# Chunk 7 of the attention scored inside the key/value loop, with the cached keys, score banks, buffers and ScalarE's order set for it

## The chip, the cores and the metric

The kernel runs on one core of a Trainium2 chip. The metric is the device time of one launch in microseconds. The engines named below are TensorE (PE in the profile, its weight loads PEld), VectorE (DVE), ScalarE (ACT), GpSimd (POOL) and SyncE (SP, which here only issues DMAs). Each engine works through its own list of instructions in order; between engines, semaphores order the work.

## The reference

One inference step of a two-layer model over 1024 prompt rows and 32 sample rows of width 1024. Layer 0 is an mLSTM mixer, layer 1 attention in a band of chunks; each is followed by an MLP. The change touches the place where layer 1 begins: keys and values are computed once from the stream, and each chunk of 64 queries attends to its own chunk and the eight before it, with a learned bias by relative position.

```python
kv = (x * (1 + kv_scale) + kv_shift) @ p['w_kv']
k_sh = kv[..., :KV_W].reshape(Bsz, S, NKV_B, HD_B)
v_sh = kv[..., KV_W:].reshape(Bsz, S, NKV_B, HD_B)
q = (u @ p['w_q_b'][lb]).reshape(Bsz, S, NH_B, HD_B)
...
def one_chunk(args):
    ci, qb = args
    kb = lax.dynamic_slice_in_dim(kp, ci * CHUNK, span, axis=1)
    vb = lax.dynamic_slice_in_dim(vp, ci * CHUNK, span, axis=1)
    s = jnp.einsum('bqkgd,bskd->bkgqs', qb, kb).astype(jnp.float32) * (HD_B ** -0.5) + bias
    valid = (ci * CHUNK - BAND + jnp.arange(span)) >= 0
    s = jnp.where(valid, s, -jnp.inf)
    p = jax.nn.softmax(s, axis=-1).astype(vb.dtype)
    return jnp.einsum('bkgqs,bskd->bqkgd', p, vb)
```

There are 16 query heads in 4 key groups of 4. The 32 sample rows attend to 512 cached keys and their own 32.

## The kernel before

**Precision.** Products are taken on values split into a high and a low part (hi and lo); ScalarE writes the hi part by a rounding cast, VectorE the lo part as a difference (`split`, L89 and L90).

**The key/value loop.** `for t in range(NT)` runs over 9 blocks of rows: 8 of 128 prompt rows and one of the 32 sample rows (t = 8). For each block, `kv_input(t)` loads the normed rows from DRAM (L1728), scales and shifts them on GpSimd (L1733) and VectorE (L1734) and splits them into `uk_t` (L89, L90). Two blocks are always prepared ahead. TensorE then multiplies: 24 matmuls for the keys (`kv0_t`) and 24 for the values (`kv1_t`), three at a time (L1755 hi by hi, L1756 hi by lo, L1757 lo by hi), into banks of PSUM that `bank()` hands out in rotation.

**Keys into place.** `put_keys` takes a block of keys: it splits them (`kd`, L1702 ScalarE, L1703 VectorE), then, at the next tick of the `flow`, transposes them on TensorE (`kt`, L1708, four matmuls into one bank) and copies them to the two forms of the key buffer `k` (L1713; four copies on ScalarE, then four on VectorE). New keys are named kt_n, the cached ones kt_c. `cached_keys(c)` loads a block of 128 cached keys and values, yields, and hands over to `put_keys`; the loop adds one of its four blocks at t = 0, 2, 4 and 6. `flow` is a list of such generators, and `flow.tick()`, called twice a block, moves them on. For t >= 4 the block's keys and values are also written out (`ks`, L1766 to L1770).

**The attention.** Only after the loop are the bias tiles loaded (bias0 to bias3, L1787 and L1791), and the order of work is a list, `todo`: for each pair of key groups `gp`, chunks alternate between wide ones (9 chunks of keys) and slim ones, beginning with chunk 8, then 7, 12, 6. Each entry is a `Group` of one chunk and one key group `e`. A group has two units (two query heads of 64 queries each make 128 rows). A unit is: scores on TensorE (`s`, L1805), the bias added and the row's extreme taken on VectorE (L1815, then a read of its accumulator), exp on ScalarE (L1818). Then per group a reciprocal of the sums (L1824 VectorE), the two units normalized on GpSimd (L1826), their transposes on TensorE (`pt`, L1840) and copies to `pT` that alternate between ScalarE (L1849) and VectorE (L1851). When both groups of a chunk are there, `pv` multiplies by the values (L1862), and the result goes back, split again, into `QO` (L1867, L1868).

In round n of the loop, group n is scored, group n - 1 normalized, group n - 3 transposed and group n - 4 multiplied by the values. Two score buffers rotate (tag `s`, `bufs=2`), three for `pt`, one for `pv`. TensorE's order in this loop is as written (`manual_schedule`); elsewhere, and on the other engines, a scheduler orders the instructions by its own estimate, within what the data and the buffers allow. Softmax tiles `p` take their place from three pools in a rotation of 12 counted by `nun`; the x tiles of `kv_input` use one of these pools (`raw_tile`) too.

## Time and profile before

| | |
|---|---|
| median of 3 runs | 2427.9 us (2427.4 to 2428.0) |
| profiled execution | 2430.0 us, its span 2427.9 us |
| TensorE's clock, mean over the span | 0.993 of full |
| key/value loop, from block 2 to the last transposes | about 1361 to 1411 us of the span |
| attention begins with the scores of chunk 8 | 1412.4 us |

Times in the profile are counted from the span's start. A row of the windows view gives, for a stretch, the busy microseconds of PE, PEld, DVE, ACT and POOL with the number of instructions in brackets, then the granted TensorE clock, the busy share of the DMA engines and GB/s. A row of the timeline gives start, duration, engine, line, operation, output and inputs, how many instructions it sums up, and in square brackets the idle time before it with what ended it. A row of the waits view gives who waited for whom: microseconds in total, times, longest. A row of the groups view gives the count, busy us and mean ns of one, then the idle time of the engine just before.

### The profile page before, as it was taken

The numbers are of one execution on the slowest core, as the hardware profiler recorded it, in microseconds if no ns is written. First come the engines' busy times: TensorE is split into PE (matmuls) and PEld (weight loads), VectorE is DVE, ScalarE is ACT, GpSimd is POOL, SyncE is SP. The second block draws the span as 40 slices with busy tenths as digits, with TensorE's granted clock in tenths as the row PEclk, the third lists the DMA queues.
The fourth block names the chain that finished last, engine by engine and source line by source line (L and its number), as shares of the span: only waits on it lengthen the run. The fifth ranks groups of instructions, "written<-read, shape, count | busy, mean of one in ns | idle before, by whom it ended". The sixth has DMA issues, their size and how long they took to land.

```text
span 2427.9 us, 44306 instructions
## 1 busy us (share of the span) xinstructions
PE 2361.4 (97%) x17180; PEld 2265.5 (93%) x17180; DVE 1973.8 (81%) x4094; ACT 1180.5 (49%) x2394; POOL 166.5 (7%) x315
## 2 busy tenths in 40 slices
PE   7999999999999999999999999999999999899997
PEld 4999999999999999999989977789999999899997
DVE  4899897778788789989887666756998888887878
ACT  4544456278566630000147466764776777222212
POOL 0111100000000000000001124420000000000003
PEclk9999999999999999999999999999999999999999
DMA  8432322436556896576413220042586779966642
GB/s 295 124 112 87 108 81 90 161 109 206 183 184 203 290 345 244 211 263 216 162 62 100 69 70 1 10 121 57 168 279 222 257 259 337 367 245 235 228 149 72
DMA packets 283702, 423.60 MB, mean 174 GB/s; under 512 B 15320, under 2 KB 205164, under 8 KB 278372
## 3 DMA queue, kind: packets, MB, share of 16 engines
q1 hardware_dynamic: 279460, 390.50, 48.3%
q10 hardware_dynamic: 4032, 30.28, 3.1%
q8 instruction: 135, 2.21, 0.4%
q14 instruction: 75, 0.61, 0.1%
HBM read 304.91 MB, written 118.17 MB: 174 GB/s over the span
## 4 chain that ended last, share of the span: by engine, by line
PE 50%; DVE 10%; DMA 4%; ACT 4%; issue 2%; POOL 1%; SPq 0%; ACTq 0%; DVEq 0%; POOLq 0%
PE dn L1424 11%; PE up L1289 8%; PE dn L120 4%; PE dn L119 4%; PE dn L118 4%; PE pv L1862 3%; PE s L1805 2%; PE pt L1840 2%; DMA radw<-in_w_ada_dram 2%; PE op_b L118 1%; PE op_b L119 1%; DVE wf_u L90 1%; PE op_b L120 1%; DMA rdn_u<-in_w_up_dram 1%; PE up L120 1%
## 5 line engine op out<-in xcount | busy, mean ns | idle before, releaser
L1054 DVE SCALAR_TENSOR_TENSOR ACX<-dn,ada,ACX 128x264 f32<-128x264 f32 (+6 forms) x664 | 281.5, 447 | 84.6 <-PE dn L1424 41.3
L1424 PE MATMUL dn<-fx,wf_d 128*128 128x264 f32 x2016 | 254.0, 285 | 6.4 <-DVE ACX L1054 4.0
L1424 PEld LDWEIGHTS dn<-fx,wf_d 128*128 128x128 f32 x2016 | 248.7, 188 | 8.7 <-DVE ACX L1054 2.7
L89 ACT CAST w_dn<-raw_dn 128x1024 fp32r<-128x1024 f32 x36 | 37.7, 1051 | 284.0 <-DMA raw_dn<-in_w_down_dram 133.1
L118 PE MATMUL dn<-hs,w_dn 128*128 128x384 f32 (+2 forms) x512 | 161.0, 315 | 0.0
L119 PE MATMUL dn<-hs,w_dn 128*128 128x384 f32 (+2 forms) x512 | 160.9, 315 | 0.0
L120 PE MATMUL dn<-hs,w_dn 128*128 128x384 f32 (+2 forms) x512 | 156.4, 314 | 1.3 <-DVE w_dn L90 1.3
L1289 PE MATMUL up<-TF,wf_u 128*128 128x264 f32 x1056 | 143.4, 285 | 3.8 <-ACT H L1292 3.8
L1289 PE MATMUL up<-U,wf_u 128*128 128x264 f32 x1056 | 140.1, 285 | 2.5 <-DVE H L1295 2.0
L1289 PE MATMUL up<-u,wf_u 128*128 128x264 f32 x1056 | 139.7, 285 | 1.6 <-ACT wf_u L89 0.6
L277 DVE SCALAR_TENSOR_TENSOR aw<-radw,cs,aw 128x512 f32<-128x512 f32 x196 | 139.3, 743 | 0.8 <-DMA radw<-in_w_ada_dram 0.8
L1289 PEld LDWEIGHTS up<-TF,wf_u 128*128 128x128 f32 x1056 | 134.2, 188 | 5.1 <-ACT H L1292 5.1
L1289 PEld LDWEIGHTS up<-U,wf_u 128*128 128x128 f32 x1056 | 133.1, 188 | 4.0 <-DVE H L1295 3.0
L1289 PEld LDWEIGHTS up<-u,wf_u 128*128 128x128 f32 x1056 | 132.6, 188 | 2.5 <-ACT wf_u L89 0.8
L119 PE MATMUL dn<-U,w_dn 128*128 128x384 f32 (+2 forms) x416 | 129.8, 313 | 0.0
L118 PE MATMUL dn<-U,w_dn 128*128 128x384 f32 (+2 forms) x416 | 129.4, 312 | 0.3 <-DVE ada L302 0.3
L120 PE MATMUL dn<-U,w_dn 128*128 128x384 f32 (+2 forms) x416 | 125.5, 312 | 0.6 <-DVE w_dn L90 0.6
L120 PEld LDWEIGHTS dn<-hs,w_dn 128*128 128x128 f32 x512 | 95.9, 188 | 2.1 <-DVE w_dn L90 1.7
L119 PEld LDWEIGHTS dn<-hs,w_dn 128*128 128x128 f32 x512 | 96.5, 188 | 0.0
L118 PEld LDWEIGHTS dn<-hs,w_dn 128*128 128x128 f32 x512 | 96.4, 188 | 0.1
L1815 DVE CUSTOM_DVE_ANT_0 p<-s,bias 128x576 f32<-128x576 f32 (+9 forms) x132 | 79.1, 605 | 20.2 <-PE s L1805 13.4
L90 DVE TENSOR_TENSOR HL<-H,HL 128x1056 fp32r<-128x1056 f32 x64 | 80.3, 1254 | 17.5 <-ACT HL L89 17.5
(394 smaller groups left out, 7167.5 us busy)
## 6 DMA issues: line engine op xcount, KB each, us to landing
hpl<-HL SPq DMA_DIRECT2D x144, 264.0 KB
rdn_u<-in_w_up_dram SPq DMA_DIRECT2D x64, 512.0 KB
hd<-HL SPq DMA_DIRECT2D x28, 1056.0 KB
fx<-hd SPq DMA_DIRECT2D x50, 528.0 KB
radw<-in_w_ada_dram SPq DMA_DIRECT2D x24, 1024.0 KB
hd<-HM SPq DMA_DIRECT2D x28, 792.0 KB
raw_up<-in_w_up_dram SPq DMA_DIRECT2D x40, 512.0 KB
raw_dn<-in_w_down_dram SPq DMA_DIRECT2D x36, 512.0 KB
```

The lines of the kernel that those rows point to most:

```text
L90: (eng or nc.vector).tensor_sub(dst_l, src, dst_h.bitcast(F32))
L118: nc.tensor.matmul(ps, wh, mov(0, k), start=(k == 0), stop=False)
L119: nc.tensor.matmul(ps, wh, mov(1, k), start=False, stop=False)
L120: nc.tensor.matmul(ps, wl, mov(0, k), start=False, stop=(k == nk - 1))
L277: nc.vector.scalar_tensor_tensor(acc[cnd], raw[:, k], sc, acc[cnd], op0=ALU.mult, op1=ALU.add)
L1054: nc.vector.scalar_tensor_tensor(xs, ps[:, off + o:off + o + mm_], gate[:, fc, cnd:cnd + 1], xs, op0=ALU.mult, op1=ALU.add)
L1289: nc.tensor.matmul(p, self.ws[w][:, wl, k], moving(f, tp, xl, k), start=first and k + n_ == 0, stop=k == 3 and n_ == 2, skip_group_check=n ...
L1424: nc.tensor.matmul(p, ws[w][:, wl, k], t[:, s0, xl], start=first and k + n_ == 0, stop=k == kg - 1 and n_ == 2, skip_group_check=not first)
L1805: nc.tensor.matmul(s[:, b, :w], qst, kk[i][:, g, k0 + j0:k0 + j0 + w], start=(i == 0), stop=(i == 1))
L1815: nc.vector.tensor_tensor_reduce(out=z.rearrange("p (b w) -> p b w", b=np_), in0=s[:, :np_, :w], in1=bt.rearrange("p (b w) -> p b w", b=np ...
L1840: nc.tensor.transpose(pt[:kp, j - j0, pr * P:(pr + 1) * P], ps_[pr][:, j * P:j * P + kp], ident)
L1862: nc.tensor.matmul(pv[64 * e:64 * e + 64, :nq], V[:kp, vt0 + j, g * 64:(g + 1) * 64], pts[e][:kp, j, :nq], start=(j == 0), stop=(j == nt - 1))
```

## The change

Chunk 7 becomes the first entry of `todo`, ahead of chunk 8, and its two groups are scored inside the key/value loop: group 0 ahead of block 7's matmuls and group 1 ahead of block 8's, through `early`. Their scores go to PSUM banks of the loop (`bank`), and their bias comes from two new tiles (`near_bias`), loaded at t = 6 into buffers of `raw_tile`. Group 0 is normalized in the second call. After the loop the rounds start at n = 2.

```diff
-        yield 3.0
+        yield 4.0
         yield from put_keys(cr, P, TP + t * P, f"c{t}")
...
+    nun, near, groups = [7], {}, {}
+    bank_n[0] += 6
...
+        s = bank(f"s_{nm}")[:, None] if near else psT.tile([P, 2, 512], F32, tag="s", name=f"s_{nm}", bufs=2)
...
+            bt = near[self.e][:, pr] if near else \
+                bias[2 * self.g + pr][:, 576 - self.nk:] if self.c < 16 else sbias[self.g]
...
+            if not gp and i < 2:
+                c = 7 + i
...
+    def near_bias(e):
+
+        b = raw_tile([P, 2, 512], f"near_{e}")
+        for hd in range(2):
+            nc.sync.dma_start(b[64 * hd:64 * hd + 64],
+                              bias_d[4 * e + hd:4 * e + hd + 3:2, :, 64:576].rearrange("h i j -> i h j"))
+        return b
+
+    def early(n):
+
+        groups[n] = Group(*todo[n][:3])
+        for pr in range(2):
+            groups[n].scores(pr)
+        if n:
+            normalize(groups[0].units, groups[0].mx)
+
     for t in range(NT):
-        if t % 2 == 0 and t < 8:
-            flow.add(cached_keys(t // 2))
+        if t in (0, 1, 3, 4):
+            flow.add(cached_keys((0, 1, 3, 4).index(t)))
+        if t >= NT - 2:
+            early(t - NT + 2)
...
+        if t == NT - 3:
+            near.update({e: near_bias(e) for e in range(2)})
+        if t >= NT - 3:
+            bias_load(t - NT + 3)
     flow.finish()
+    near.clear()
+    nun[0] = 4
     ps0.__exit__(None, None, None)
+    bias_load(3)
...
     with tc.manual_schedule(engines={mybir.EngineType.PE}):
-        for n in range(len(todo) + 4):
-            new, old, done = n if n < len(todo) else None, groups.get(n - 3), groups.pop(n - 4, None)
-            if done and done.e:
+        act_order = tc.manual_schedule(engines={mybir.EngineType.PE, mybir.EngineType.Activation})
+        act_order.__enter__()
+        for n in range(2, len(todo) + 4):
+            if n == 6:
+                act_order.__exit__(None, None, None)
+            new, done = n if n < len(todo) else None, groups.pop(n - 4, None)
+            old = groups.get(n - 2 if n < 4 else n - 3) if n != 4 else None
+            if done and done.e and n > 5:
                 done.values()
             if new is not None:
                 groups[n] = Group(*todo[n][:3])
                 groups[n].scores(0)
+            if n == 4:
+                groups[1].values()
```

The functions of the attention (`softmax_unit`, `normalize`, `transposed`, `weighted_values`, `Group`) are moved as they stand to a place ahead of the loop, and the loads of the bias tiles become `bias_load(i)`, three of which are called at t = 6, 7 and 8. The cached keys are taken up at t = 0, 1, 3 and 4, with a yield of 4.0 in place of 3.0. `bank_n[0] += 6` shifts the rotation of the banks, and `nun` starts at 7 and is set to 4 after the loop, with which the softmax tiles of chunk 12 and later take the same pools as before. In rounds 2 to 5 ScalarE's order too is as written. The matmuls of the attention and of the loop are the same in number and shape.

VectorE's list around the third and fourth block of keys, before (kd1 is the lo part of a key block, c for cached and n for new, the number the block; k1 the copies to the second key buffer; uk and x the loop's inputs by block):

```order
L1734 TENSOR_TENSOR x1_5_15192<-x1_5_15192,kvss_14864 128x1024
L90 TENSOR_TENSOR uk_3_15024<-x1_3_15022,uk_3_15024 128x1024
L1703 TENSOR_TENSOR kd1_n2_15110<-kv0_2_15029,kd0_n2_15109 128x256
L1713 CAST k1_14842<-kt_c0_15055 64x2x128 x4
L1713 CAST k1_14842<-kt_n1_15068 64x2x128 x4
L1703 TENSOR_TENSOR kd1_c1_15185<-ck_1_15081,kd0_c1_15184 128x256
L90 TENSOR_TENSOR uk_4_15115<-x1_4_15113,uk_4_15115 128x1024
```

and now:

```order
L1734 TENSOR_TENSOR x1_5_15211<-x1_5_15211,kvss_14864 128x1024
L90 TENSOR_TENSOR uk_3_15026<-x1_3_15024,uk_3_15026 128x1024
L1703 TENSOR_TENSOR kd1_c0_15058<-ck_0_14914,kd0_c0_15057 128x256
L1713 CAST k1_14842<-kt_n1_15061 64x2x128 x4
L1703 TENSOR_TENSOR kd1_n2_15113<-kv0_2_15031,kd0_n2_15112 128x256
L90 TENSOR_TENSOR uk_4_15118<-x1_4_15116,uk_4_15118 128x1024
L1713 CAST k1_14842<-kt_c0_15099 64x2x128 x4
```

The lo part of the cached block c0, which stood several rows ahead of x1_5, now stands behind the split of uk_3, and its copies follow two rows later than those of n1. On TensorE the transposes kt_c0 stood between block 2's key and value matmuls; they now stand directly ahead of block 3's first matmul.

TensorE's list where the loop ends and the attention begins, before (kt_n8 is the last key block, s_0_8_00 the scores of group pair 0, chunk 8, group 0, unit 0):

```order
L1708 MATMUL kt_n8_15634<-ident_64,kd0_n8_15626 128x32 x2
L1708 MATMUL kt_n8_15634<-ident_64,kd1_n8_15627 128x32 x2
L1805 MATMUL s_0_8_00_15675<-k0_14841,QO1_14267 128x288
L1805 MATMUL s_0_8_00_15675<-k1_14842,QO1_14267 128x288
...
L1805 MATMUL s_0_8_01_15683<-k0_14841,QO1_14267 128x288
...
L1805 MATMUL s_0_8_10_15692<-k0_14841,QO1_14267 128x288
...
L1805 MATMUL s_0_7_10_15728<-k0_14841,QO1_14267 128x512
L1805 MATMUL s_0_7_10_15728<-k1_14842,QO1_14267 128x512
L1840 MATMUL pt_0_8_0_0_15738<-ident_64,p_0_8_00_15680 128x128
```

and now:

```order
L1708 MATMUL kt_n8_15685<-ident_64,kd0_n8_15670 128x32 x2
L1708 MATMUL kt_n8_15685<-ident_64,kd1_n8_15671 128x32 x2
L1776 MATMUL s_0_8_00_15712<-k0_14841,QO1_14267 128x288
L1776 MATMUL s_0_8_00_15712<-k1_14842,QO1_14267 128x288
...
L1811 MATMUL pt_0_7_0_0_15724<-ident_64,p_0_7_00_15506 128x128
L1811 MATMUL pt_0_7_0_0_15724<-ident_64,p_0_7_01_15512 128x128
...
L1776 MATMUL s_0_8_01_15730<-k0_14841,QO1_14267 128x288
...
L1811 MATMUL pt_0_7_0_2_15738<-ident_64,p_0_7_00_15506 128x128
```

Before, seven score units stood ahead of the first transposes; now the transposes of chunk 7 stand between the score units of chunk 8.

VectorE's list at the same place, before:

```order
L1703 TENSOR_TENSOR kd1_n8_15627<-kv0_8_15549,kd0_n8_15626 32x256
L1713 CAST k1_14842<-kt_c3_15575 64x2x128 x4
L1713 CAST k1_14842<-kt_n7_15588 64x2x128 x4
L1713 CAST k1_14842<-kt_n8_15634 64x2x32 x4
L1815 ISA p_0_8_00_15680,mx_0_8_0_15674<-s_0_8_00_15675,bias0_15654 128x576
L1815 ISA mx_0_8_0_15674 128x1
L1815 ISA p_0_8_01_15688,mx_0_8_0_15674<-s_0_8_01_15683,bias0_15654 128x576
```

and now:

```order
L1786 ISA p_0_7_10_15594,mx_0_7_1_15590<-s_0_7_10_15591,near_1_15496 128x512
...
L1786 ISA p_0_7_11_15600,mx_0_7_1_15590<-s_0_7_11_15597,near_1_15496 128x512
...
L1795 RECIPROCAL mx_0_7_1_15590<-mx_0_7_1_15590 128x2
L1703 TENSOR_TENSOR kd1_n8_15671<-kv0_8_15606,kd0_n8_15670 32x256
L1713 CAST k1_14842<-kt_n7_15632 64x2x128 x4
L1713 CAST k1_14842<-kt_n8_15685 64x2x32 x4
L1786 ISA p_0_8_00_15717,mx_0_8_0_15711<-s_0_8_00_15712,bias0_15499 128x576
```

The copies of the cached block c3 have left this place for an earlier one, and the reads of chunk 7's last scores now stand ahead of the last key block's lo part.

More of the change, by code (lines that the diff above doesn't have):

```diff
@@ L1743, in cached_keys, with bias_load @@
         nc.sync.dma_start(V[:, 8 + t], cv[t * P:(t + 1) * P])
-        yield 3.0
+        yield 4.0
         yield from put_keys(cr, P, TP + t * P, f"c{t}")
-    for t in range(NT):
-        if t % 2 == 0 and t < 8:
-            flow.add(cached_keys(t // 2))
-        m = P if t < NT - 1 else TS
-        uk = uks[t]
-        pk = [bank(f"kv{i}_{t}")[:, :256] for i in range(2)]
-        for i in range(2):
-            for k in range(KC):
-                w = wkv[i][k // 4]
-                nc.tensor.matmul(pk[i], uk[:, 0, k], w[:, 0, k % 4], start=(k == 0), stop=False)
-                nc.tensor.matmul(pk[i], uk[:, 0, k], w[:, 1, k % 4], start=False, stop=False)
-                nc.tensor.matmul(pk[i], uk[:, 1, k], w[:, 0, k % 4], start=False, stop=(k == KC - 1))
-            if i == 0:
-                flow.tick()
-        vi = t if t < NT - 1 else 12
-        nc.scalar.copy(V[:m, vi], pk[1][:m])
-        flow.add(put_keys(pk[0][:m], m, t * P if t < NT - 1 else TP + 512, f"n{t}"))
-        flow.tick()
-        if t >= 4:
-            ks = tmp_t([P, 256], f"ks_{t}")
-            nc.scalar.copy(ks[:m], pk[0][:m])
-            dk, dv = (o["k_p"], o["v_p"]) if t < NT - 1 else (o["k_s"], o["v_s"])
-            r0 = (t - 4) * P if t < NT - 1 else 0
-            nc.sync.dma_start(dk[0, r0:r0 + m].rearrange("s g d -> s (g d)"), ks[:m])
-            nc.sync.dma_start(dv[0, r0:r0 + m].rearrange("s g d -> s (g d)"), V[:m, vi])
-        if t + 2 < NT:
-            uks.append(kv_input(t + 2))
-    flow.finish()
-    ps0.__exit__(None, None, None)
     at_cm = tc.tile_pool(name="attn", bufs=1, reuse_waits="tile")
     at = at_cm.__enter__()
-    psT_cm = tc.tile_pool(name="psT", bufs=1, space=PSUM, reuse_waits="tile")
-    psT = psT_cm.__enter__()
     bias, sbias = [], []
-    for i, (nb, ns) in enumerate(((3, 0), (3, 0), (2, 1), (0, 3))):
+    def bias_load(i):
+        nb, ns = ((3, 0), (3, 0), (2, 1), (0, 3))[i]
         bt = ring.tile([P, 2112], F32, tag="wc", name=f"bias{i}", bufs=6)
@@ L1792, in trunk_kernel @@
                               bias_d[h0:h0 + 4 * ns - 3:4, :32, :544].rearrange("h i j -> i h j"))
-        bias += [b3[:, j] for j in range(nb)]
-        sbias += [s3[:, j] for j in range(ns)]
-    nun = [0]
+        bias.extend(b3[:, j] for j in range(nb))
+        sbias.extend(s3[:, j] for j in range(ns))
+    nun, near, groups = [7], {}, {}
+    bank_n[0] += 6
     def softmax_unit(qst, g, k0, nk, bt, off, mx, nm):
-        s = psT.tile([P, 2, 512], F32, tag="s", name=f"s_{nm}", bufs=2)
+        s = bank(f"s_{nm}")[:, None] if near else psT.tile([P, 2, 512], F32, tag="s", name=f"s_{nm}", bufs=2)
         parts = [(0, 0, nk)] if nk <= 512 else [(0, 0, nk // 2), (1, nk // 2, nk // 2)]
@@ L1888, in scores @@
                 return
-            bt = bias[2 * self.g + pr][:, 576 - self.nk:] if self.c < 16 else sbias[self.g]
+            bt = near[self.e][:, pr] if near else \
+                bias[2 * self.g + pr][:, 576 - self.nk:] if self.c < 16 else sbias[self.g]
             self.units.append(softmax_unit(qo(self.c)[:, self.e, self.gp, pr * P:(pr + 1) * P], self.g, self.k0, self.nk,
@@ L1920, in trunk_kernel @@
             c = slim[gp][i // 2] if i % 2 else wide[i // 2] if i < 16 else slim[gp][8]
+            if not gp and i < 2:
+                c = 7 + i
             todo += [(gp, c, e, gp and e and i in (8, 11)) for e in range(2)]
-    groups = {}
-    with tc.manual_schedule(engines={mybir.EngineType.PE}):
-        for n in range(len(todo) + 4):
-            new, old, done = n if n < len(todo) else None, groups.get(n - 3), groups.pop(n - 4, None)
-            if done and done.e:
+    def near_bias(e):
[4 more added lines that the diff above has]
+        return b
@@ new lines, in early @@
+    def early(n):
[4 more added lines that the diff above has]
+            normalize(groups[0].units, groups[0].mx)
+    for t in range(NT):
+        if t in (0, 1, 3, 4):
+            flow.add(cached_keys((0, 1, 3, 4).index(t)))
+        if t >= NT - 2:
+            early(t - NT + 2)
+        m = P if t < NT - 1 else TS
+        uk = uks[t]
+        pk = [bank(f"kv{i}_{t}")[:, :256] for i in range(2)]
+        for i in range(2):
+            for k in range(KC):
+                w = wkv[i][k // 4]
+                nc.tensor.matmul(pk[i], uk[:, 0, k], w[:, 0, k % 4], start=(k == 0), stop=False)
+                nc.tensor.matmul(pk[i], uk[:, 0, k], w[:, 1, k % 4], start=False, stop=False)
+                nc.tensor.matmul(pk[i], uk[:, 1, k], w[:, 0, k % 4], start=False, stop=(k == KC - 1))
+            if i == 0:
+                flow.tick()
+        vi = t if t < NT - 1 else 12
+        nc.scalar.copy(V[:m, vi], pk[1][:m])
+        flow.add(put_keys(pk[0][:m], m, t * P if t < NT - 1 else TP + 512, f"n{t}"))
+        flow.tick()
+        if t >= 4:
+            ks = tmp_t([P, 256], f"ks_{t}")
+            nc.scalar.copy(ks[:m], pk[0][:m])
+            dk, dv = (o["k_p"], o["v_p"]) if t < NT - 1 else (o["k_s"], o["v_s"])
+            r0 = (t - 4) * P if t < NT - 1 else 0
+            nc.sync.dma_start(dk[0, r0:r0 + m].rearrange("s g d -> s (g d)"), ks[:m])
+            nc.sync.dma_start(dv[0, r0:r0 + m].rearrange("s g d -> s (g d)"), V[:m, vi])
+        if t + 2 < NT:
+            uks.append(kv_input(t + 2))
+        if t == NT - 3:
+            near.update({e: near_bias(e) for e in range(2)})
+        if t >= NT - 3:
+            bias_load(t - NT + 3)
@@ new lines, in trunk_kernel @@
+    flow.finish()
+    near.clear()
+    nun[0] = 4
+    ps0.__exit__(None, None, None)
+    bias_load(3)
+    psT_cm = tc.tile_pool(name="psT", bufs=1, space=PSUM, reuse_waits="tile")
+    psT = psT_cm.__enter__()
+    with tc.manual_schedule(engines={mybir.EngineType.PE}):
+        act_order = tc.manual_schedule(engines={mybir.EngineType.PE, mybir.EngineType.Activation})
[6 more added lines that the diff above has]
+            if done and done.e and n > 5:
```

## The prediction

> **What bounds the kernel now.** I read first the page's busy shares:

> ```profile
> PE 2361.4 (97%) x17180; PEld 2265.5 (93%) x17180; DVE 1973.8 (81%) x4094; ACT 1180.5 (49%) x2394; POOL 166.5 (7%) x315
> ```

> TensorE is busy for 97% of the span, so a change that leaves its work alone can win only where it idles or where its clock is not full. The change issues the same attention matmuls as before; only their places differ. So I looked for idle and slow clock near those places, in windows of 3.41 us laid on the steps at which the granted clock changes (PE, PEld, DVE, ACT, POOL busy with counts, then the clock, DMA share and GB/s):

> ```profile
> 1368.53:1371.94 3.41, 1.65 (x14) 1.45 (x13) 3.35 (x6) 1.57 (x3) 0.00 (x0) 1.00 0.04 9
> 1371.94:1375.36 3.42, 3.42 (x19) 3.42 (x18) 3.32 (x8) 0.37 (x1) 0.06 (x1) 0.50 0.55 151
> ...
> 1409.49:1412.90 3.41, 1.88 (x17) 1.67 (x16) 3.27 (x10) 2.21 (x9) 0.00 (x0) 1.00 0.43 70
> 1412.90:1416.32 3.42, 3.42 (x15) 2.95 (x13) 2.64 (x9) 1.74 (x4) 0.00 (x0) 0.50 0.92 211
> 1416.32:1419.73 3.41, 1.82 (x6) 0.90 (x6) 1.83 (x6) 2.03 (x5) 1.48 (x2) 1.00 1.04 240
> 1419.73:1423.14 3.41, 3.41 (x15) 2.83 (x13) 1.84 (x8) 2.34 (x7) 1.47 (x3) 0.50 1.07 252
> 1423.14:1426.56 3.42, 0.96 (x8) 0.75 (x8) 1.43 (x4) 2.23 (x6) 2.73 (x4) 1.00 0.27 57
> 1426.56:1429.97 3.41, 3.41 (x18) 2.79 (x18) 1.87 (x4) 0.95 (x2) 0.00 (x0) 0.50 0.00 0
> ...
> 1569.92:1573.33 3.41, 2.49 (x18) 1.59 (x18) 1.91 (x9) 2.55 (x8) 2.42 (x4) 1.00 0.00 0
> 1573.33:1576.75 3.42, 3.42 (x30) 3.25 (x30) 3.34 (x11) 2.78 (x9) 1.06 (x6) 1.00 0.00 0
> ```

> The entry to attention, 1409.49 to 1429.97, holds three such pairs. Idle: (3.41 - 1.88) + (3.41 - 1.82) + (3.42 - 0.96) = 5.6 us. Slow clock: (3.42 + 3.41 + 3.41) / 2 = 5.1 us. Together 10.7 us, and the view of waits names what the idle time waited for:

> ```profile
> PE pt L1840 <- POOL p L1826: 2.5, 1, 2.5
> PE s L1805 <- DVE mx L1815: 1.6, 2, 0.8
> PE s L1805 <- DVE k L1713: 1.5, 1, 1.5
> ```

> The 1.5 is the first score matmul waiting for the last key copies to leave a PSUM bank, the 1.6 two waits for a score buffer that VectorE has not read, and the 2.5 the first transposes waiting for the first softmax. They are the start of a pipeline with nothing yet to fill it.

> **The change part by part.** *The entry, what is removed.* Chunk 7 is now scored inside the key/value loop and its four softmax units are through VectorE, ScalarE and, for the first half, GpSimd before the loop ends. Its transposes are then ready work between the scores of chunk 8, and the first score tile stands on a bank that the last key copies do not hold. The three waits lose their causes: -10.7 us if no window falls to half.

> *The entry, what is left.* VectorE still has to read four score tiles. What TensorE does until then, and how long VectorE takes, from the steady rounds (timeline of PE, then groups from 1430 to 1613 us):

> ```profile
> 1432.72 0.60 PE L1840 MATMUL pt<-ident,p 128*128 128x128 f32 x4
> 1433.07 0.77 PE L1805 MATMUL s<-k,QO 128*128 128x288 f32 x4
> 1433.68 0.60 PE L1840 MATMUL pt<-ident,p 128*128 128x128 f32 x4
> ```

> ```profile
> L1826 POOL TENSOR_SCALAR p<-p,mx 128x576 f32<-128x576 f32 x60 | 44.1, 749 | 56.4 <-DVE mx L1824 56.4
> L1815 DVE CUSTOM_DVE_ANT_0 p<-s,bias 128x576 f32<-128x576 f32 x58 | 43.6, 753 | 3.2 <-PE pt L1840 1.4 <-PE s L1805 0.7
> L1851 DVE COPY pT<-pt 128x512 f32<-128x512 f32 x38 | 26.0, 683 | 0.9 <-PE pt L1840 0.4
> L1815 DVE DVE_READ_ACCUMULATOR2_ANT mx<- 128x1 f32 x120 | 9.9, 82 | 0.0
> L1824 DVE RECIPROCAL mx<-mx 128x2 f32<-128x2 f32 x59 | 9.7, 164 | 17.6 <-ACT p L1818 17.1
> ```

> By their starts a score unit takes TensorE 1433.68 - 1433.07 = 0.61 us and a pair of transposes 1433.07 - 1432.72 = 0.35. After the last key transposes TensorE has five score units and four pairs before it needs chunk 7's second pT in its first pv: 5 x 0.61 + 4 x 0.35 = 4.5 us. VectorE's queue up to that pT holds the new row's key copies, four reads, two pT copies and a reciprocal:

> ```profile
> 1408.80 1.73 DVE L1713 CAST k<-kt_c 64x256 fp32r<-64x256 f32 x4 [1.12 <-ACT k L1713]
> 1410.54 2.69 DVE L1713 CAST k<-kt_n 64x256 fp32r<-64x256 f32 x8
> 1410.45 0.43 PE L1708 MATMUL kt_n<-ident,kd_n 32*128 32x32 f32 x4
> ```

> The eight casts take 2.69 us, a block's four alone 1.73, so the new row's four take 0.96. The queue is 0.96 + 4 x (0.753 + 0.082) + 2 x 0.683 + 0.164 = 5.8 us, 1.3 more than TensorE's 4.5. That holds if VectorE stands free when the last transposes are done. Before, block 7's casts still ran to 1410.54 + 1.73 = 1412.27 there, 1.4 us after 1410.45 + 0.43; in the change the cached block's 1.73 us is out of their way, but two reads of chunk 7 lie there instead, so I take the middle of 1.3 and 2.7: 2.0 us. Two later waits of a pipeline still short are likely, for a bank of chunk 12's scores (a read, 0.84 at most) and for chunk 8's second normalize on GpSimd (0.75 at most); half of each is 0.8. Left over: 2.8 us, spread in pieces under 1.7, so no window should halve. Bounds: 0 (copies and reads hidden behind TensorE) and 5.6 (every microsecond of the old idle comes back, without its clock). ScalarE's fixed order costs nothing by itself: in the windows above it is busy at most 2.34 of 3.41 us.

> *The third block of keys.* Cached keys now come in at blocks 0, 1, 3 and 4, and tick four units late. The keys c0 move behind the split of uk_3 on VectorE and their transposes from the middle of block 2 to its end. TensorE already stands there:

> ```profile
> 1368.11 1.23 DVE L1734 TENSOR_TENSOR x<-x,kvss 128x1024 f32<-128x1024 f32 x1 [4.18 <-POOL x L1733]
> 1369.25 1.22 DVE L90 TENSOR_TENSOR uk<-x,uk 128x1024 fp32r<-128x1024 f32 x1
> 1370.50 0.42 DVE L1703 TENSOR_TENSOR kd_n<-kv,kd_n 128x256 fp32r<-128x256 f32 x1
> ```

> ```profile
> 1364.63 0.60 PE L1708 MATMUL kt_c<-ident,kd_c 128*128 128x128 f32 x4
> 1365.07 0.60 PE L1708 MATMUL kt_n<-ident,kd_n 128*128 128x128 f32 x4
> 1368.37 0.28 PE L1755 MATMUL kv<-w_kv,uk 128*128 128x256 f32 x1
> 1368.49 0.28 PE L1756 MATMUL kv<-w_kv,uk 128*128 128x256 f32 x1
> 1370.53 0.39 PE L1757 MATMUL kv<-w_kv,uk 128*128 128x256 f32 x1 [1.76 <-DVE uk L90]
> ```

> The stall ended with uk_3's split. Now it ends with c0's difference behind that split (0.42, the kd_n row's shape), and on its far side then lie the transposes kt_c0 (1365.07 - 1364.63 = 0.44) and block 3's first two matmuls (2 x 0.12 by their starts), which ran ahead of it before. Added: 0.42 + 0.44 + 0.24 = 1.1 us. The window behind it is at half clock either way. Bounds: 0 (uk_3 comes as much earlier), and 1.1 + 1.7 = 2.8 (the longer stall empties parts of two windows).

> *The moved scores and their bias.* Chunk 7's eight score matmuls leave the entry for the loop: what they add there they took there, 0. Their VectorE reads, four of at most 0.84 us, lie where VectorE has room: it was busy 1.09 of 3.41 us in the window 1406.08 to 1409.49:

> ```profile
> 1406.08:1409.49 3.41, 3.41 (x31) 3.41 (x31) 1.09 (x3) 2.52 (x7) 0.00 (x0) 1.00 0.92 243
> ```

> Their bias comes in two new tiles of 512 KB, four DMAs of 256 KB on SP's queue, held until block 6's and block 7's splits release the buffers. A 512 KB tile of this queue took:

> ```profile
> 1361.87 0.53 SPq L1728 DMA_DIRECT2D x<-xsp  x1
> 1366.17 1.91 POOL L1733 TENSOR_TENSOR x<-x,kvss 128x1024 f32<-128x1024 f32 x1 [6.72 <-DMA x<-xsp]
> 1394.18 1.23 DVE L90 TENSOR_TENSOR uk<-x,uk 128x1024 fp32r<-128x1024 f32 x1
> 1407.26 0.41 DVE L1703 TENSOR_TENSOR kd_n<-kv,kd_n 32x256 fp32r<-32x256 f32 x1 [1.90 <-ACT kd_n L1702]
> ```

> 1366.17 - 1361.87 = 4.3 us. Block 7's split ends at 1394.18 + 1.23 = 1395.4, so the later tile lands near 1400; its readers stand just ahead of the last kd_n, which started at 1407.26. Two reads of 0.84 before that give 1405.6: 5 to 6 us in hand, cost 0. The large bias tiles still queue behind the outputs of blocks 7 and 8 as SP's order had them before; 0 as well, with the bounds of the entry.

> **Sum**: -10.7 + 2.8 + 1.1 + 0 = -6.8 us. The profiled execution took 2430.0 us (span 2427.9), which gives 2423.2; the median of the runs shown is 2427.9, 2.1 us lower, so the forecast for it is 2421.1.

> **The rivals.**
> 1. *The windows fall otherwise.* Where TensorE's left-over 2.8 us lands as half of one window, one more window is at half clock: +1.7, 2422.8. Where block 3's stall straddles an edge with less than half in either, that one disappears: -1.7, 2419.4. The entry stands about 1.1 us plus the moved scores' 2 us later against the edges, so neither is excluded; against a large spread speaks that three runs lie within 0.6 us, under one window's price. [...]
> 2. *The wait moves into VectorE's queue.* The casts of block 7, behind two reads and a late ScalarE, hold up the reads of chunk 8; the entry keeps all 5.6 us of idle, and one half window, and block 3 costs 2.8: -10.7 + 5.6 + 1.7 + 2.8 = -0.6, 2427.3. For it: VectorE is in order and was the releaser of two of the three waits. Against: its queue of 5.8 us against 4.5.
> 3. *The near bias comes late, slower.* VectorE stands at chunk 7's last reads until the second bias tile lands; kd_n8, the casts of block 7 and TensorE's last key transposes queue behind it. TensorE has block 8's 48 matmuls to do meanwhile, 48 x 0.12 = 5.8 us, so it decides only from about 5 + 5.8 = 11 us of lateness. Past that, 8.3 us of idle with two half windows costs 11.7: 2421.1 + 11.7 = 2432.8. Against: it needs a 512 KB transfer of some 24 us where one took 4.3.
> 4. *More than forecast.* Both left-over terms at their lower bounds: 2427.9 - 10.7 = 2417.2.

> **How the numbers follow.** Forecast 0.62; windows later 0.12 and earlier 0.10; VectorE's queue 0.07; late bias 0.05; more 0.04. A measurement of this kernel can tell 0.2%, 4.9 us, from no change: faster means under 2423.0, slower over 2432.8. Of the forecast's 0.62, whose own range is 2419.0 to 2423.5, 0.56 lies under 2423.0; of rival 1's upper case half. Faster: 0.56 + 0.06 + 0.10 + 0.04 = 0.76; same: 0.06 + 0.06 + 0.07 = 0.19; slower 0.05. The range 2417.5 to 2425.5 holds the forecast and rival 1, and leaves out rivals 2, 3 and most of 4, 0.16.

> **What would show it.** Right: the windows of the entry at clock 1.00, with no wait of scores on k and none of some 2.5 us of transposes on GpSimd; a stall of some 2.8 us before block 3, now ended by kd_c (L1703), not by uk (L90); chunk 7's 128x512 scores inside the loop without idle before them. Wrong: a clock of 0.50 after 1409; kt_n8 waiting for kd_n8 or VectorE for a near tile's DMA; pv waiting over 2 us for pT; a second slow window near block 3.

## The result, and the profile after

The changed kernel takes 2419.4 us (median of 8 runs, 2418.2 to 2426.1); the kernel before took 2427.65 us (median of 8, 2425.0 to 2432.3). The ratio is 0.9967 with a 95% interval of 0.9956 to 0.9979, that is 5 to 11 us less. Forecast was 2421.1, range 2417.5 to 2425.5.

Medians of runs that spread over 7 us say little about terms of 1 us. So everything below is measured inside one trace, between two points that every kernel has: the start of **block 2's first key matmul** and the start of **chunk 13's first pv**, in the first pair of key groups. Before, they lie at 1361.40 and 1455.01 us, 93.6 us apart; in the changed kernel at 1357.34 and 1442.91, 85.6 us apart. The difference is 8.0 us. The changed execution is already 4.1 us ahead at the first point. The kernel before itself reaches that point at 1357.28 us in its second trace, so this part of the 11 us between the two spans is the spread of executions and not the change.

The windows of the changed kernel, at block 3 and over the entry (PE, PEld, DVE, ACT, POOL busy, then clock, DMA share, GB/s):

```profile
1364.31:1367.72 3.41, 1.04 (x9) 1.04 (x10) 3.35 (x6) 1.46 (x3) 0.00 (x0) 1.00 0.02 3
1367.72:1371.13 3.41, 3.41 (x18) 3.41 (x18) 3.34 (x7) 1.32 (x4) 0.00 (x0) 0.50 0.61 157
...
1408.68:1412.09 3.41, 2.84 (x23) 2.43 (x22) 2.95 (x10) 1.35 (x6) 0.00 (x0) 1.00 1.06 253
1412.09:1415.51 3.42, 3.23 (x24) 2.62 (x25) 2.19 (x7) 3.40 (x9) 0.00 (x0) 1.00 1.06 245
1415.51:1418.92 3.41, 3.40 (x23) 2.25 (x24) 2.29 (x8) 1.85 (x5) 2.82 (x4) 1.00 1.07 237
1418.92:1422.33 3.41, 2.86 (x22) 2.28 (x21) 3.20 (x9) 2.74 (x7) 1.29 (x5) 1.00 0.44 91
```

In the entry the idle time is 0.57 + 0.19 + 0.01 + 0.55 = 1.3 us where it was 5.6, and no window is at 0.50 where three were. Block 3 keeps its pair of windows, a half-empty one and a slow one. The waits of TensorE from 1355 to 1440 us (in total, times, longest):

```profile
PE kt_c L1708 <- DVE kd_c L1703: 2.6, 1, 2.6
PE s L1776 <- DVE mx L1786: 0.8, 2, 0.6
PE pt L1811 <- ACT pT L1820: 0.4, 1, 0.4
PE pv L1833 <- ACT pT L1820: 0.2, 1, 0.2
```

The waits on k (1.5) and on GpSimd (2.5) are gone, those on VectorE's reads are down from 1.6 to 0.8, and block 3's stall now ends with kd_c. The moved pieces, in TensorE's timeline:

```profile
1394.08 0.60 PE L1708 MATMUL kt_c<-ident,kd_c 128*128 128x128 f32 x4
1394.43 1.17 PE L1776 MATMUL s<-k,QO 128*128 128x512 f32 x4
1395.44 0.28 PE L1924 MATMUL kv<-w_kv,uk 128*128 128x256 f32 x1
...
1401.61 1.09 PE L1776 MATMUL s<-k,QO 128*128 128x512 f32 x4
1402.54 0.28 PE L1924 MATMUL kv<-w_kv,uk 128*128 128x256 f32 x1
```

They stand between key matmuls without a gap, and take 0.35 (the last cached block's transposes, which the loop had later), 1.01 and 0.93 us by their starts: 2.3 us that left the stretch behind block 8's first matmul. That first matmul splits the 8.0 us: up to it (the loop) the stretch grew from 42.3 to 45.2, 0.6 us more than the moved 2.3; behind it (the entry), it shrank from 51.3 to 40.4, 8.6 us more than the moved 2.3.

### The profile page after: what moved, and what is told of

Read it like the earlier page. It is cut to its first block, busy times and chain, and to the rows that moved or that the text cites. A ratio compares the mean times of both kernels' runs of the same rounds, so it can differ in the third digit from the quotient of the medians.

```text
span 2416.9 us, 44321 instructions
## 1 busy us (share of the span) xinstructions
PE 2355.8 (97%) x17180; PEld 2261.8 (94%) x17180; DVE 1974.4 (82%) x4094; ACT 1180.1 (49%) x2394; POOL 166.4 (7%) x315
## 3 DMA queue, kind: packets, MB, share of 16 engines
q8 instruction: 135, 2.21, 0.4%
## 4 chain that ended last, share of the span: by engine, by line
PE 52%; DVE 9%; ACT 4%; DMA 3%; issue 1%; POOL 0%; SPq 0%; DVEq 0%; ACTq 0%; POOLq 0%
PE dn L1424 11%; PE up L1289 9%; PE dn L120 5%; PE dn L119 5%; PE dn L118 5%; PE pv L1833 3%; PE s L1776 2%; PE pt L1811 2%; DMA rdn_u<-in_w_up_dram 1%; PE op_b L118 1%; PE op_b L119 1%; PE op_b L120 1%; DVE wf_u L90 1%; PE up L120 1%; PE up L118 1%
## 5 line engine op out<-in xcount | busy, mean ns | idle before, releaser
L1054 DVE SCALAR_TENSOR_TENSOR ACX<-dn,ada,ACX 128x264 f32<-128x264 f32 (+6 forms) x664 | 282.4, 448 | 86.6 <-PE dn L1424 42.3
L90 DVE TENSOR_TENSOR HL<-H,HL 128x1056 fp32r<-128x1056 f32 x64 | 80.4, 1256 | 17.1 <-ACT HL L89 16.9
L1789 ACT ACTIVATE p<-p,mx 128x576 f32<-128x576 f32 (+9 forms) x132 | 86.5, 656 | 15.4 <-DVE mx L1786 15.1
```

The lines of the kernel that those rows point to most:

```text
L90: (eng or nc.vector).tensor_sub(dst_l, src, dst_h.bitcast(F32))
L1054: nc.vector.scalar_tensor_tensor(xs, ps[:, off + o:off + o + mm_], gate[:, fc, cnd:cnd + 1], xs, op0=ALU.mult, op1=ALU.add)
L1789: nc.scalar.activation(z, z, AF.Exp, bias=mx[:, 0:1], scale=-1.0, accum_out=mx[:, 1:2])
```

## The experiments

All lengths are of the stretch above. The table gives them first, with the two inner points and the windows at half clock inside.

| kernel | block 2 to block 8 | to chunk 8's first score | to chunk 13's first pv | windows at 0.50 |
|---|---|---|---|---|
| before | 42.3 | 51.0 | 93.6 | 4 (block 3, three in the entry) |
| before, second trace | 42.1 | 50.7 | 93.4 | 3 (entry) |
| swap_only | 42.0 | 54.1 | 93.7 | 2 (entry) |
| ck_only | 44.7 | 51.6 | 91.2 | 2 (block 3) |
| changed | 45.2 | 51.8 | 85.6 | 1 (block 3) |
| changed, second trace | 45.1 | 51.8 | 85.7 | 1 (block 3) |
| ck_old | 44.1 | 52.3 | 85.9 | 1 (block 3) |
| bank0 | 45.3 | 52.7 | 85.8 | 1 (block 3) |
| nun_on | 44.6 | 51.6 | 85.9 | 0 |
| act_free | 45.1 | 51.7 | 89.8 | 3 (block 3, two in the entry) |
| near_late | 46.8 | 53.5 | 87.2 | 1 (block 3) |
| dv3 | 43.6 | 50.2 | 84.1 | 0 |
| pool_add5 | 40.7 | 47.4 | 80.9 | 0 |
| pool_add | 40.7 | 47.4 | 81.1 | 0 |

### Is it the early scores, or only the order of the chunks?

**swap_only**: the kernel before, with chunk 7 first in the list.

```diff
             c = slim[gp][i // 2] if i % 2 else wide[i // 2] if i < 16 else slim[gp][8]
+            if not gp and i < 2:
+                c = 7 + i
```

> The kernel before with chunk 7 put ahead of chunk 8 in the list and nothing else: chunk 7 is still scored after the loop. Same stretch (before 93.6, with the change 85.6). Theory: the entry's three waits come from the empty pipeline, whichever chunk is first; 93 to 94 us, three windows at half clock in the entry. Rival: what helps is that the short chunk with one score matmul pair per unit goes first; 88 us or less.

93.7 us, two windows at half clock. TensorE waits 1.5 us on k, as before, and 2.2 on VectorE's reads (1.6 before); the transposes' wait of 2.5 has only changed its releaser, to VectorE's pT copies (1.6) and GpSimd (0.8). The order of the chunks alone is worth nothing in this trace. That the early scores carry the gain is not isolated by any run: none scores chunk 7 early and leaves the rest of the kernel before as it was.

One part of the change has no run at all, the earlier start of the second large bias tile (issued 47.8 and 48.5 us after block 2's first matmul, before 49.7 and 51.0). In the kernel before, chunk 8's fourth unit needs that tile. TensorE had started the last of its matmuls by 1416.01, but VectorE's list has the read behind two reads of chunk 7:

```profile
1417.12 0.69 DVE L1815 CUSTOM_DVE_ANT_0 p<-s,bias 128x512 f32<-128x512 f32 x1 [0.75 <-PE s L1805]
...
1418.64 0.69 DVE L1815 CUSTOM_DVE_ANT_0 p<-s,bias 128x512 f32<-128x512 f32 x1 [0.83 <-PE s L1805]
...
1419.26 0.75 DVE L1815 CUSTOM_DVE_ANT_0 p<-s,bias 128x576 f32<-128x576 f32 x1
```

That unit's score buffer, one of two, was thus held for some 3 us (1416.01 to the read's start at 1419.26). In the changed kernel the fourth read of chunk 8 comes fourth. How much of the 1.6 us of waits on VectorE's reads is this order, and not the empty pipeline, stays open.

### Or the cached keys?

**ck_only**: the kernel before, with only the cached keys moved.

```diff
-        yield 3.0
+        yield 4.0
...
-        if t % 2 == 0 and t < 8:
-            flow.add(cached_keys(t // 2))
+        if t in (0, 1, 3, 4):
+            flow.add(cached_keys((0, 1, 3, 4).index(t)))
```

> The kernel before with only the cached keys moved to blocks 0, 1, 3 and 4 and the yield of 4.0. Same stretch (before 93.6). Theory: block 3 loses 0.3 to 0.7 us, and the entry gives at most its wait on k back, with the pipeline still empty behind it: 93 to 94.5 us. Rival: with the cached block's casts gone from the loop's end the first wait (1.5 us) and the half-clock window behind it fall away: 90.4 us, and most of the change's gain does not need the early scores.

91.2 us, between the two. The waits of TensorE from 1400 to 1440 us:

```profile
PE s L1805 <- DVE mx L1815: 3.0, 4, 1.2
PE pt L1840 <- ACT pT L1849: 2.5, 1, 2.5
PE s L1805 <- DVE k L1713: 0.2, 1, 0.2
```

The wait on k falls from 1.5 to 0.2, as the rival said, but the idle time does not: it moves to the reads and the copies, 5.7 us in all against 5.6. What fell is the number of half-clock windows in the entry, from three to none, with as much idle time. So the theory was right on the entry's idle time and wrong on the total, because it left the clock as it was. It was also wrong on the loop: block 3 was to lose 0.3 to 0.7 us and loses 2.3 (block 4 comes 19.0 us after block 2, before 16.7), since two slow windows follow its stall:

```profile
1364.72:1368.14 3.42, 1.47 (x13) 1.23 (x11) 1.92 (x2) 1.62 (x3) 1.47 (x1) 1.00 0.00 0
1368.14:1371.55 3.41, 2.58 (x12) 2.58 (x13) 3.31 (x8) 1.79 (x5) 0.00 (x0) 0.50 0.46 115
1371.55:1374.97 3.42, 3.42 (x18) 3.42 (x17) 2.74 (x6) 0.08 (x1) 0.72 (x1) 0.50 0.53 127
```

That is the case which the prediction had as its bound for block 3, put at 2.8 us: the longer stall emptying parts of two windows.

**ck_old**: the changed kernel with the cached keys as before (the same lines, reversed).

> The change with the cached keys taken up at blocks 0, 2, 4 and 6 with a yield of 3.0, as before. Measured inside the trace from block 2's first key matmul to chunk 13's first pv (before 93.6 us, with the change 85.6). Theory: the earlier cached keys cost 0.3 to 0.7 us at block 3 and bring nothing in the entry, since VectorE's queue there has slack of that size; undone, 85.0 us, and the stall before block 3 ends with the split of uk_3 again (1.8 us instead of 2.6). Rival: block c3's casts, back at the loop's end, push the casts of block 7 and the reads of chunk 8 back by 1.7 us; 87.3 us or, with a half-clock window, 89.

85.9 us: neither. Block 3's stall is 1.8 us again and the loop 1.1 us shorter (0.8 after kt_c3's 0.35 us, which go back behind it); in the entry the first score of chunk 8 waits 1.1 us for ScalarE (`V`, L1930) and the reads stand 0.9. The move of the cached keys costs in the loop what it gives in the entry, 0.3 us net, which one trace each does not tell from nothing. Beside the early scores it is worth that little; alone, in ck_only, it was worth 2.4.

### The banks, the softmax tiles and ScalarE's order

**bank0**: without the shift.

```diff
-    bank_n[0] += 6
```

> The change without the shift of the banks' rotation. Same stretch. Theory of the prediction: the shift takes the first score tile of chunk 8 off the bank that the key copies of block 7 hold; without it TensorE waits 1 to 1.5 us for k there, 86.6 to 87.1 us, or 88.8 if a window halves with it. Rival: with chunk 7 scored early the rotation stands elsewhere anyway and the shift does nothing: 85.6 us and no wait of s on k.

The wait is there, but 0.7 us (s on k), and the stretch is 85.8. The first score comes 0.9 us later and most of it is regained by the fourth, because the reads of VectorE set the pace behind it: TensorE's waits on them are 0.2 us here and 0.8 in the changed kernel. The prediction named the wait rightly and counted it as the whole 1.5 of the old trace.

**nun_on**: the counter of the softmax tiles not set to 4 after the loop.

```diff
-    nun[0] = 4
+    pass
```

> The change without the setting of the softmax tiles' counter to 4 after the loop: the rotation goes on from 11. Same stretch, and on to the last pv of pair 1, chunk 11 (before 248.7, with the change 241.0). Theory: the counter decides nothing in the entry (85.6 us), but each later unit takes another pool than before, and some meet a tile still held by weight blocks or the loop; 2 to 6 us of waits later in the attention, 243 to 247 us. Rival: any rotation of 12 does as well, 241.0 us.

85.9 us to chunk 13, then 10.4 us more than the changed kernel up to the last pv of pair 1, chunk 11 (251.4 against 241.0). TensorE's waits from 1440 to 1615 us, of this run:

```profile
PE pv L1833 <- ACT pT L1820: 6.9, 4, 4.6
PE pv L1833 <- DVE pT L1822: 1.6, 2, 1.3
```

In the changed kernel these two are 1.3 and 0.2 us. The rest is two windows at half clock, at 1563.7 and 1587.6, where ten matmuls of pv take 2.82 and 2.78 us and twenty, at 1570.79, take 2.45. At 3.41 / 2 = 1.7 us each, an estimate, they cost 3.4: 5.6 + 1.4 + 3.4 = 10.4. ScalarE's own row just ahead of the first shows the cause:

```profile
1562.14 1.04 ACT L89 CAST w_ob<-raw_ob 128x1024 fp32r<-128x1024 f32 x1 [2.49 <-DMA raw_ob<-in_w_out_b_dram]
1563.09 0.58 ACT L1820 COPY pT<-pt 128x512 f32<-128x512 f32 x1
```

The output weights' cast stands in ScalarE's list ahead of a pT copy and waits for its load; that the load was late because softmax tiles held its buffers is argued from the pools, not shown. The theory had the place and the kind right and the size too small (2 to 6): the waits alone are 7.0, and it did not count the 3.4 of the clock.

**act_free**: ScalarE left to the scheduler.

```diff
-        act_order = tc.manual_schedule(engines={mybir.EngineType.PE, mybir.EngineType.Activation})
-        act_order.__enter__()
...
-            if n == 6:
-                act_order.__exit__(None, None, None)
```

> The change without the fixed order of ScalarE in rounds 2 to 5 (TensorE's stays fixed). Stretch from block 2's first key matmul to chunk 13's first pv: before 93.6 us, with the change 85.6. Theory of the prediction: ScalarE has room there and its order costs and brings nothing: 85.6 us. Rival: left to the scheduler, ScalarE puts an exp ahead of a pT copy that the first pv or the transposes of chunk 8 wait for; 87 to 88.5 us, with a wait of TensorE on ScalarE of over 1 us.

89.8 us. ScalarE's and then TensorE's timeline:

```profile
1414.68 0.76 ACT L1789 ACTIVATE p<-p,mx 128x576 f32<-128x576 f32 x1
...
1415.56 0.77 ACT L1789 ACTIVATE p<-p,mx 128x576 f32<-128x576 f32 x1
...
1417.20 0.78 ACT L1789 ACTIVATE p<-p,mx 128x576 f32<-128x576 f32 x1 [0.77 <-DVE mx L1786]
...
1418.09 1.07 ACT L1820 COPY pT<-pt 128x512 f32<-128x512 f32 x2
```

```profile
1418.73 1.11 PE L1811 MATMUL pt<-ident,p 128*128 128x128 f32 x4 [3.04 <-ACT pT L1820]
```

All four exps of chunk 8 go first, and the two pT copies of chunk 7 come behind the last, where the fixed order has them after the first and the third exp. TensorE's transposes wait 3.0 us for a buffer, and the two windows behind are at half clock: four transposes take 1.11 us there and 0.60 ahead of the wait, and the first pv's 16 matmuls take 3.61 by their starts (1420.74 to 1424.35), where a later pv of 16 in the changed kernel takes 2.34. The rival is right, and by more than it said: 4.2 of the 8.0 us hang on ScalarE's order. The prediction's "costs nothing by itself" looked at ScalarE's share of busy time, which says nothing of what stands ahead of what.

### Had the near bias time in hand?

**near_late**: chunk 7's second bias tile loaded one block later.

```diff
-        if t == NT - 3:
-            near.update({e: near_bias(e) for e in range(2)})
+        if NT - 3 <= t < NT - 1:
+            near[t - NT + 3] = near_bias(t - NT + 3)
```

> The change with the second tile of chunk 7's bias loaded after block 7 instead of after block 6, about 5 us later. Same stretch. Theory of the prediction: it has 5 to 6 us in hand, so 85.6 us, no wait of VectorE on that load over 1 us. Rival: VectorE stands at the reads of chunk 7's second group, the lo part of the last key block queues behind it, and TensorE's last key transposes wait: 87 us or more, 89 with a half-clock window.

87.2 us, but the 1.6 more lie ahead of anything that this edit moves: at block 2 a key matmul waits 1.5 us for a split whose x came late from DRAM: GpSimd stood 2.63 us for that load and began at 1357.50, in the changed kernel it stood 0.25 and began at 1352.43. From block 3's first matmul on the lengths agree to 0.02 us (76.01 against 76.03), and no wait of VectorE on a load appears from 1396 to 1412 us. The time in hand was real.

### What is the stall before block 3?

**dv3**: VectorE's order as written while blocks 0 to 2 are set up.

```diff
+    dve_order = None
     for t in range(NT):
+        if t == 0:
+            dve_order = tc.manual_schedule(engines={mybir.EngineType.DVE})
+            dve_order.__enter__()
+        if t == 3:
+            dve_order.__exit__(None, None, None)
```

> The change with VectorE's order as written while blocks 0 to 2 are set up, so that the split of uk_3 stands ahead of the addition to x_5, which waits for a load. Same stretch (with the change 85.6). Theory: the stall before block 3 (2.6 us) is VectorE standing at that addition; it goes, with the half-clock window behind it (1.7): 81.3 to 82 us, and kv_3 has no window at 0.50. Rival: the split cannot come earlier since its buffer is held by block 1, or the addition to x_5 is then late and the stall only moves to block 4 or 5: 84.5 to 86 us.

84.1 us, 1.5 us of the 3.6 to 4.3 expected. Up to block 4 it gains 3.6 us (14.1 against 17.65 from block 2), the stall and its slow window, as the theory said. Then a stall of 1.7 us stands before block 4's third matmul, as the rival said. The test was not clean: the addition to x_5 still stood ahead of uk_3's split in VectorE's list, only other instructions had moved.

**pool_add5**: the addition to x on GpSimd from block 5 on, which takes it out of VectorE's list. **pool_add** does so for all blocks.

```diff
-        nc.vector.tensor_add(x, x, kvsh[:, :, cnd:cnd + 1].broadcast_to([P, KC, m]))
+        (nc.gpsimd if t >= 5 else nc.vector).tensor_add(x, x, kvsh[:, :, cnd:cnd + 1].broadcast_to([P, KC, m]))
```

> The change with the addition to x (L1734) on GpSimd instead of VectorE for blocks 5 to 8. Stretch from block 2's first key matmul to chunk 13's first pv: before 93.6 us, with the change 85.6. Theory: the stall before block 3 is VectorE standing at the addition to x_5, ahead of the split of uk_3; with it on GpSimd the split goes at once, the 2.6 us and the half-clock window behind it (1.7) go, and GpSimd's 2 us more per block lie within its idle time: 81.3 to 82.5 us, and the time 3 to 4 us under the change's. Rival: as when VectorE's order was set by hand, the later loads are not earlier and the stall moves to block 4 or 5: 83.5 to 85.5 us.

> The change with the addition to x on GpSimd for every block. Same stretch. Theory: as with blocks 5 to 8 alone, 81.3 to 82.5 us; the blocks ahead have time. Rival: a block's input takes some 2 us longer on GpSimd than on VectorE, which shows at blocks 2 and 3, where the input is only just there: 83 to 86 us with waits of the key matmuls on the split.

80.9 and 81.1 us: the 2.6 and the 1.7 are gone. VectorE's timeline of the changed kernel, then of pool_add5, then GpSimd's of pool_add5:

```profile
1363.93 1.23 DVE L1734 TENSOR_TENSOR x<-x,kvss 128x1024 f32<-128x1024 f32 x1 [4.24 <-POOL x L1733]
1365.07 1.22 DVE L90 TENSOR_TENSOR uk<-x,uk 128x1024 fp32r<-128x1024 f32 x1
```

```profile
1357.63 1.72 DVE L1713 CAST k<-kt_n 64x256 fp32r<-64x256 f32 x4
1359.38 1.23 DVE L90 TENSOR_TENSOR uk<-x,uk 128x1024 fp32r<-128x1024 f32 x1
1360.53 0.42 DVE L1703 TENSOR_TENSOR kd_c<-ck,kd_c 128x256 fp32r<-128x256 f32 x1
```

```profile
1361.72 1.91 POOL L1733 TENSOR_TENSOR x<-x,kvss 128x1024 f32<-128x1024 f32 x1 [6.86 <-DMA x<-xsp]
1363.71 1.91 POOL L1734 TENSOR_TENSOR x<-x,kvss 128x1024 f32<-128x1024 f32 x1
```

The split of uk_3 follows block 0's key casts at once, 2.2 us after block 2's first matmul, where it came 7.7 us after it in the changed kernel. It had only been queued behind the addition to x_5, which waited for its load (6.79 us of GpSimd's time, then 4.24 of VectorE's, in the changed kernel); GpSimd now waits for that load alone (6.86). The time is 2413.7 us (median of 5, 2413.1 to 2414.5) for pool_add5, its ratio to the kernel before 0.9946 (0.9934 to 0.9959), and 2414.7 with 0.9945 (0.9932 to 0.9959) for pool_add. The changed kernel on the same chip took 2419.9 (2417.0 to 2421.5), so pool_add5 beats both kernels. It is 6.2 us under the changed one; 4.7 of that is seen in the stretch. Behind the stretch the two traces of that chip differ by 2.0 us, which is within the spread: from chunk 13's first pv to the end all traces but nun_on's lie between 972.4 and 975.5 us.

### Second traces

> The changed kernel as it is, once more, for a second trace. Same stretch. Theory: the entry has no window at half clock wherever its edges fall, since no idle piece there is over 0.6 us; 85.6 us, give or take 0.5 there, and 1.7 less if the stall before block 3 happens to lie across an edge. Rival: the entry's full clock was luck of the edges: a window at 0.50 after the first scores of chunk 8, 87 us or more.

> The kernel before as it is, once more, for a second trace of its entry. Stretch from block 2's first key matmul to chunk 13's first pv (93.6 us in the first trace, with three windows at half clock in the entry; 91.2 us in the kernel with only the cached keys moved, with none). Theory: the entry's waits on k, on VectorE and on GpSimd are there again, 4 to 7 us, and how many windows halve behind them depends on where the edges fall, 0 to 3: 90.5 to 94 us, never near 85.6. Rival: the first trace was an unlucky one, and the entry usually loses under 3 us: under 89 us, and the change's gain is mostly luck of the edges.

The changed kernel repeats at 85.7 us, the entry at full clock, block 3 with its slow window. The kernel before repeats at 93.4 us with the same three waits (2.5, 1.6 and 1.5) and three slow windows:

```profile
1408.88:1412.30 3.42, 3.27 (x13) 2.68 (x12) 2.28 (x7) 2.04 (x5) 0.24 (x1) 0.50 0.98 246
...
1415.71:1419.12 3.41, 3.41 (x16) 3.03 (x15) 1.55 (x6) 2.50 (x8) 2.04 (x3) 0.50 1.09 243
...
1422.54:1425.95 3.41, 3.41 (x17) 2.50 (x17) 2.04 (x5) 1.35 (x3) 0.00 (x0) 0.50 0.00 0
```

Its windows fell within 0.1 us of where they had fallen, counted from block 2's first matmul (51.5 and 51.6 us to the first slow one). So it shows the loss again, but not what another place of the edges would have cost this kernel; that stays open.

## Why the prediction held, and where its terms were off

| term | forecast | measured in the trace |
|---|---|---|
| entry: waits and slow windows removed | -10.7 | the three causes gone, no slow window |
| entry: left over | +2.8 | +2.1, so that the entry has -8.6; 1.3 of it is idle time, 0.5 hides inside the first pv, 0.3 is not located |
| block 3 | +1.1 | +0.9 at block 4, +0.6 left at block 8 |
| moved scores and their bias | 0 | 0 (76.01 and 76.03 us with the load a block later) |
| sum | -6.8 | -8.0 |

*The entry* went as the steps said: the first scores do not wait for k, the transposes do not wait for GpSimd, the pieces of idle time are under 0.6 us, and nothing halves. **What was left** was put at 2.8 us, 2.0 of it for the first pv standing on VectorE's 5.8 us of work. The waits view gives that pv 0.2 us. By its starts it lost more: its 16 matmuls took 3.03 us (1414.62 to 1417.65), the next pv of 16 takes 2.34 (1436.43 to 1438.77).

```profile
1414.62 0.65 PE L1833 MATMUL pv<-pT,V 128*64 128x256 f32 x2
1415.45 2.27 PE L1833 MATMUL pv<-pT,V 128*64 128x256 f32 x14 [0.19 <-ACT pT L1820]
```

```profile
1415.25 0.69 DVE L1822 COPY pT<-pt 128x512 f32<-128x512 f32 x1
...
1415.92 0.67 DVE L1822 COPY pT<-pt 128x512 f32<-128x512 f32 x1
```

So the term was 0.7 us and not 2.0. The step that failed is "before it needs chunk 7's second pT": the first pv takes its four key blocks in order, and the first two of that pT come from ScalarE's copy; VectorE's copy feeds the last two and ended, at 1416.59, while the pv ran. The rest of VectorE's lag shows as a 0.57 us wait for a score buffer.

*Block 3* was priced at 0.42 + 0.44 + 0.24. The stall's end did move by about 0.3 behind uk_3, but only half of kt_c0 lay beyond it:

```profile
1363.71 0.38 PE L1708 MATMUL kt_c<-ident,kd_c 128*128 128x128 f32 x2
1366.68 0.44 PE L1708 MATMUL kt_c<-ident,kd_c 128*128 128x128 f32 x2 [2.59 <-DVE kd_c L1703]
1366.88 0.36 PE L1924 MATMUL kv<-w_kv,uk 128*128 128x256 f32 x1
```

The two transposes of the hi part ran before the stall, so 0.20 and not 0.44 us were added there.

*The large bias tiles* were counted as no cost. No wait of TensorE names them, but there was less room than I thought: chunk 8's last read waited 1.0 us for its tile, and the two pT copies above stand behind that read in VectorE's list.

```profile
1414.56 0.76 DVE L1786 CUSTOM_DVE_ANT_0 p<-s,bias 128x576 f32<-128x576 f32 x1 [1.01 <-DMA bias<-bias_d]
```

*ScalarE's order* was counted as nothing too. As a cost that is right, but the forecast rests on it: without it the gain is 3.8 us and not 8.0 (93.6 - 89.8).

*Rivals.* The edges that rival 1 counts with are seen: in the trace of the kernel before, all 16 steps of the granted clock from 20.27 to 1429.97 us lie whole multiples of one length apart, 1409.70 / 413 = 3.41 us, and in the changed kernel's the 10 from 19.46 to 2064.05 do, 2044.59 / 599 = 3.41. The windows did fall otherwise in two traces. nun_on lost 2.5 us at the same stall without a slow window behind it and came to block 4 1.8 us earlier (15.9 against 17.65); the second trace of the kernel before came there 1.9 us earlier than its first (14.8 against 16.7). That is the 1.7 that rival 1 had, but it does not last: at block 8 0.6 and 0.3 us of it are left, and nun_on's stretch to chunk 13 is no shorter (85.9 against 85.6). The second trace of the kernel before shows 1.3 us of it spent in a second wait for a split, behind block 4; where nun_on lost it was not followed. The late bias and the wait in VectorE's queue did not come.

## What to carry to other kernels

At the start of this pipeline the first waits were worth more than their length: three windows with TensorE busy for 1.88, 1.82 and 0.96 us of 3.41 were each followed by one at half clock, 5.6 us of idle time with three slow windows behind it that cost some 4.4. So look for work that is ready earlier and put it between the first steps; here the order in which the same work starts was worth nothing by itself (93.7 us against 93.6). When such work is moved, look at each engine's list around it: here 4.2 of the 8.0 us hung on ScalarE's copies not standing behind four exps. A stall that ends with an instruction is not always that instruction's: see what stands ahead of it in its engine's list, since the split that TensorE waited for started 7.7 us after block 2's first matmul, queued behind an addition that waited for a load, and 2.2 us after it with that addition on GpSimd.

## What the runs showed that I had not expected

As much idle time came with another clock: ck_only has 5.7 us of idle in the entry and no window at half, the kernel before 5.6 us and three. So these two traces give the price of a slow window. From block 8's first matmul to chunk 13's first pv the kernel before takes 51.3 us and ck_only 46.5, 4.7 less. Of that 0.35 is kt_c3, which moved into the loop. The three slow windows thus cost about 4.4 us where 3 x 1.7 = 5.1 was counted. Its whole stretch is only 2.4 us shorter because the loop gave 2.3 back.

A slow window was also followed by another although it was not half empty: in ck_only behind 2.58 us busy of 3.41, where in the kernel before a window at full clock with 2.49 us busy (1569.92 to 1573.33) was followed by one at full clock. GpSimd took 1.91, 2.02 and 2.77 us for the addition of blocks 5 to 7 in pool_add5, VectorE 1.22 to 1.23 for the same three in the changed kernel.
